# A due-time ranking in the planner, and a down projection that takes two units in turns and reads two PSUM banks at once

## The chip, the cores and the metric

The kernel runs on one core of a Trainium2 chip. The metric is the time of one execution on the device in microseconds (us). Before the change it is 1962.56 us, the median of 3 runs (1949.43 to 1962.99).

## What is computed

One layer of a hybrid decoder, in fp32, for a prompt of 1024 tokens and 8 single-token samples (1032 columns together). Cut to what matters here:

```
h = RMSNorm(x);  q_a, kv_a, g_a, u_c, q_m, g_m = split(h @ w_in)
y_a = (sum of gated compressed, selected and window attention) @ w_o_nsa
y_b = silu(LayerNorm(causal_conv31(glu(u_c)))) @ w_o_conv
y_m = softmax(qm @ k_mem) @ v_mem @ w_o_mem
x   = x + (gm[0]*y_a + gm[1]*y_b + gm[2]*y_m) @ w_out
u, v = split(RMSNorm(x) @ w_ffn_up)             # 1024 -> 2 x 2816
y   = x + (gelu(causal_conv3(u)) * v) @ w_ffn_down   # 2816 -> 1024
```

It returns y for prompt and samples, and the new cache rows and states.

## The kernel before

**Arithmetic.** Every large product is made of three TensorE matmuls: an operand is split into a high and a low part (`wh`, `wl` of a weight; `G1h`, `G1l` and so on of an activation), and `mm3` adds wh·xh, wh·xl and wl·xh in one PSUM bank. A split costs a copy that rounds (`wh`, mostly on ACT) and a subtraction (`wl`, on DVE or POOL). DVE is VectorE, ACT ScalarE, POOL GpSimd, SP the engine that issues most DMAs.

**The planner.** No instruction is issued where it stands in the code. Class `Plan` records each with what it reads and writes (`record`; `record_any` for those that may run on DVE or POOL, or on ACT or POOL), and `flush` places them: a list scheduler with modelled costs. On each engine it looks at the operations that are ready within 30 ns (SP: 60 ns) of the earliest, and takes the one with the lowest `(prio, n)`. `prio` is the number of the instruction in the program, or, in prompt attention, one that a unit was given with a lead. For an operation with a choice of engines, `first` and `finish` choose the engine on which it would end earlier. The model knows that POOL instructions and DVE instructions with two inputs in SBUF keep each other out (`port`, `held`). The engines then run their lists strictly in order. All instructions of the compute engines carry the line of the helper, L95 (`record`) or L126 (`record_any`), so a profile is read by tile names.

**Stages** (us in the profiled execution): norms and input projections to 262; memory attention, compression and the samples' attention to 730; prompt attention to 1002; a reload of three tiles to 1042; output projections to 1240; FFN norm and the start of the up projection to 1306; up projection to 1690; the passage to the down projection to 1717; down projection to 1952; stores to 1959.

**Up and down projection** use Strassen-Winograd products: a unit of output columns is computed by seven products named 1 to 7. In the up projection the 22 units are 11 of `u` (the gate path, whose short convolution and GELU make the tile `ua`) and 11 of `v`. `take_u` does the convolution of a `u` unit on DVE.

**The down projection** has 6 groups of 4, 4, 4, 4, 4 and 2 blocks of the 2816 rows, and in each 4 units of 256 output columns: 24 units, one after the other, with the products in the order "1265734". A product is two pieces of 258 columns, each in a PSUM bank of its own: 6 matmuls to a piece in the first five groups, 3 in the last. Products 1, 6, 7, 4 accumulate in banks A (two pairs in turns), 5 and 3 in B, 2 in C. After each piece an eviction adds its 258 columns to the sum `acc` in SBUF, or, where `acc` is still empty, copies them (ACT). The raw weights of a unit come by one DMA into one of two buffers (`raw_load`), the load for unit n+1 being issued at product 5 of unit n; `w_prep` makes the sums of weight blocks (`s`, `raw<-raw`) and the splits 8 products ahead (`DNL`). Meanwhile `g_prep` makes the 14 tiles G1h to G7l of the next group (1032 columns each) out of `rA` and `rB`, which are read back from DRAM (`gD`), with `tmp` between. At a group's end `xr`, half a tile of the residual, is added to `acc`; in the last group the halves of `acc` go to `o_y`.

Of the kernel before, what the change touches and what calls it, by code (L numbers as in the profile page):

```python
# [2 lines left out]

# [4 lines left out]
F = mybir.dt.float32  # L8
# [12 lines left out]
TH = 516  # L21
# [25 lines left out]
class Plan:  # L47
# [4 lines left out]
           ("PE", "PE"): 0}  # L52

    def __init__(self):
        self.on, self.opt, self.prio, self.count = False, False, None, 0
        self.acc, self.new, self.wait, self.free, self.done = {}, [], {}, {}, []

    @staticmethod
# [3 lines left out]
    def box(self, x):  # L62

        t, ap, off = x.tensor, x.ap, x.offset
        if "DRAM" in str(x.space):
            return t.name, (0, 1, off, off + 1 + sum((n - 1) * abs(s) for s, n in ap)), None
        if t.name not in self.at:
            return t.name, (0, 128, 0, 512), None
        s0 = ap[0][0]
        start, end = self.at[t.name]  # L70
        p, f = off // s0, start + off % s0
        return "sbuf", (p, p + ap[0][1], f, f + 1 + sum((n - 1) * abs(s) for s, n in ap[1:])), (start, end, t.name)
# [20 lines left out]
    def record(self, eng, method, f, a, k):  # L93
        o = Op()
        o.eng, o.fn, o.n, o.opt = eng, (lambda: f(*a, **k)), self.count, self.opt  # L95
        o.prio = self.count if self.prio is None else self.prio
        self.count += 1
        o.deps = {}
        outs = [a[0] if a else k["out"]]
        if "accum_out" in k:  # L100
            outs.append(k["accum_out"])
        if method == "tensor_tensor_reduce":
            outs.append(a[7])
        ins = [x for x in list(a[1:7]) + [v for n, v in k.items() if n not in ("out", "accum_out")] if self.is_ap(x)]
        if "in_offset" in k:
            ins.append(k["in_offset"].ap)
        for x in ins:
            self.touch(o, *self.box(x), False)
        for x in outs:
            self.touch(o, *self.box(x), True)  # L110
        if eng == "PE":
            self.touch(o, "group " + a[0].tensor.name, (0, 1, 0, 1), None, k.get("start", True))
# [15 lines left out]
    def table(self, eng, fn):  # L128

        o = Op()  # L130
        o.eng, o.fn, o.n, o.opt, o.prio, o.deps, o.ns, o.lat, o.alts, o.port = eng, fn, self.count, False, self.count, {}, 1300.0, 0, None, False
        self.count += 1
        self.touch(o, "table", (0, 1, 0, 1), None, True)
        self.new.append(o)
# [35 lines left out]
    def flush(self):  # L170
# [3 lines left out]
        for o in self.new:  # L174
            o.left = len(o.deps)
            for q in o.deps:
                users.setdefault(q, []).append(o)
            if not o.left:
                self.enter(o)
        n = len(self.new)  # L180
        while n:
            best = None
# [29 lines left out]
            for u in users.pop(o, ()):  # L212
                u.left -= 1
                if not u.left:
                    self.enter(u)

    @staticmethod
    def port(e, o):
# [114 lines left out]
class Banks:  # L333


    def __init__(self, pool):
        self.all = [pool.tile([128, 512], F, name=f"bank{i}") for i in range(8)]
        self.turn = {}

    def use(self, **names):  # L340
        self.names = {k: [self.all[i] for i in v] for k, v in names.items()}

    def __call__(self, name):
        i = self.turn.get(name, -1) + 1
# [4 lines left out]
def drain(g):  # L349
    for _ in g:  # L350
        pass
# [33 lines left out]
FP, GSB, OTB, CVP = 0.0, 3, 4, 8e5  # L385
AH, BP = 2.5, 4.0
SLK = {'PE': 30.0, 'ACT': 30.0, 'DVE': 30.0, 'POOL': 30.0, 'SP': 60.0}
GP = (2, 5, 8, 11, 14, 17, 20)
HE, LE, UPL, DNL = "ap", "vp", 3, 8
ORD = (7, 6, 5, 4, 3, 2, 1, 0)  # L390
RB, RW, TB, VB, KH = 3, 3, 2, 2, 'p'
# [2 lines left out]
def _body(tc, nc, d, top):  # L394
# [187 lines left out]
    wo_ids = [add_chunk(d.wo[m], 10) for m in range(8)]  # L582
    wout_ids = [[add_chunk(d.wout[m], 8) for m in range(8)] for _ in range(2)]


    mh = xp_.tile([128, 8, 256], R, name="mh")
    ml = xp_.tile([128, 8, 256], R, name="ml")
# [252 lines left out]
    flush()  # L840
    gp2.close()


    oS = cp.tile([128, NB, 8], F, name="oS")

# [553 lines left out]
    drain(side())  # L1399
    bp.close()  # L1400


    oD = dp.tile([4, 128, T], F, name="oD")
    q4 = Scope(arena, "q4")
# [184 lines left out]
    plan.prio = None  # L1589
    q4.close()  # L1590


    e1, ep = Scope(arena, "e1"), Scope(arena, "ep")
    table("sigmoid_and_others")
# [54 lines left out]
    gp5.close()  # L1649
    e1.close()  # L1650


    xs, wp, xb, us, wx, v1 = [Scope(arena, n) for n in ("x2", "wp", "xb", "us", "wx", "v1")]
    X2 = [xs.tile([128, 8, TH], F, name=f"x2{h}") for h in range(2)]
# [65 lines left out]
    yp.close()  # L1720
    rw.close()

# [17 lines left out]
    units = [("u", p) if v == 0 else ("v", p) for p in range(11) for v in range(2)]  # L1740
    dgroups = [(0, 4), (4, 4), (8, 4), (12, 4), (16, 4), (20, 2)]
    units += [("d", j, p) for j in range(len(dgroups)) for p in range(4)]
    PR, PD = "1267453", "1265734"
    seq = [(n, p) for n in range(2) for p in "12"] + [(0, "6"), (1, "6")] + [(n, p) for n in range(2) for p in PR[3:]]
    seq += [(n, p) for n in range(2, len(units)) for p in (PR if n < NU else PD)]

    def raw_load(n):
        u = units[n]
# [17 lines left out]
    def w_prep(j):  # L1766

        n, p = seq[j]
        if n not in raws:
            raw_load(n)  # L1770
        r = raws[n]
        k = r[0, 0].shape[1]
        s1 = (s1t[n % 2] if n < NU else s1t[0][:, n % 2 * 256:])[:, :k * 128].rearrange("p (c m) -> p c m", m=128)
        if p == "6":
            add(s1, r[1, 0], r[1, 1], OP.add)
            add(r[1, 0], r[0, 0], r[1, 0], OP.subtract)
            add(r[0, 0], s1, r[0, 0], OP.subtract)
        elif p == ("7" if n < NU else "5"):
            if n + 1 < len(units) and n + 1 not in raws:
                raw_load(n + 1)  # L1780
        elif p == "3":
            add(r[0, 1], r[0, 1], r[0, 0], OP.subtract)
        src_ = {"1": r[0, 0], "2": r[0, 1], "6": r[0, 0], "5": s1, "3": r[0, 1], "7": r[1, 0], "4": r[1, 1]}[p]
        if units[n][0] == "d":
            i = wst["slot"]
            wst["slot"] += 1
            i, q = i // 2, i % 2 * 2
        else:
            i, q = wst["slot"] // 2, 0
            wst["slot"] += 2  # L1790
        if i not in slot:
            slot[i] = [rp.tile([128, 4, 128], R, name=nm, bufs=5) for nm in ("wh", "wl")]
        h, l = [x[:, q:q + k] for x in slot[i]]
        split_(h, l, src_)
        w_tiles["s", j] = (h, l)

    def product(j, B, lead):
        n, p = seq[j]
        while wst["prep"] < min(j + lead + 1, len(seq)):
            w_prep(wst["prep"])  # L1800
            wst["prep"] += 1
        wh, wl = w_tiles.pop(("s", j))
        k = wh.shape[1]
        if p == "1":
            bk[n] = {b: [bank(b) for _ in range(2)] for b in "ABC"}
        ps = bk[n][{"1": "A", "6": "A", "7": "A", "4": "A", "5": "B", "3": "B", "2": "C"}[p]]
        for x in range(2):
            o = ps[x][:, :TP_]
            for y in range(k):
                mm3(o, wh[:, y], wl[:, y], B[p][0][:, y, pieces[x]], B[p][1][:, y, pieces[x]],  # L1810
                    y == 0 and p in "152", y == k - 1 and p in "432", skip_group_check=p != "2")
            yield x, o

    bk = {}
    bank.use(A=(0, 1, 2, 3), B=(4, 5), C=(6, 7))
    fs = Scope(arena, "fs")
    FS = fs.tile([128, 22, NB, 3], F, name="FS")
    UO = fs.tile([128, 22, 2], F, name="UO")
# [153 lines left out]
    g_load(0, 1)  # L1972
    drain(g_prep(0))
    j = nup
    for g in range(len(dgroups)):
# [4 lines left out]
        for p in range(4):  # L1980
            for q in range(7):
                if p * 7 + q in GP:
                    next(ahead, None)
                P = seq[j][1]
                for x, ps in product(j, {q: [v[:, :dgroups[g][1] // 2] for v in w] for q, w in GB[g % 2].items()}, DNL):
                    def o(i, h):
                        return acc[2 * p + i][:, h * TH + x * TP_:h * TH + (x + 1) * TP_]
                    t_ = {"1": ((0, 0),), "2": ((0, 0),), "6": ((0, 1),), "7": ((1, 1),), "4": ((1, 0),), "5": ((1, 1),), "3": ((0, 1),)}[P]
                    for i, h in t_:
                        if g == 0 and P in "1654":  # L1990
                            act.activation(o(i, h), ps, AF.Copy)
                        else:
                            vec.tensor_tensor(o(i, h), o(i, h), ps, op=OP.add)
                j += 1
            if p == 3:
                drain(ahead)
            if 0 < g < 5:
                m, h = 2 * p + (g - 1) // 2, (g - 1) % 2
                x_ = xr[p % 2]
# [167 lines left out]
```

## Time and profile before

| | |
|---|---|
| runs | 1949.43, 1962.99, 1962.56 us; median 1962.56 |
| profiled execution | 1960.58 us; its span 1958.8 us; mean granted TensorE clock 0.982 of full speed |
| busy in the span | TensorE 95%, its weight loads 91%, DVE 78%, ACT 47%, POOL 37% |
| chain that ended last, by line | TensorE's own matmuls 36%, DVE's additions into `acc` 3%, no other over 1% |
| DMA | 212.74 MB, 109 GB/s in the mean |

The span is what the profiler saw of one execution, from its first to its last instruction; 1.8 us of that execution's time lie outside it. Busy shares are means over stages with different limits, so the views by stage below say more. In a row, "out<-in" are the program's tile names (numbers left out), "partitions x elements" the size, and a wait in brackets is idle time before an instruction and what ended it.

### The profile page before, as it was taken

What the parts mean: (1) busy time and instruction counts of PE and PEld (TensorE: products, weight loads), DVE (VectorE), ACT (ScalarE), POOL (GpSimd) and SP (SyncE); (2) the same over time, 40 slices, a digit from 0 to 9 for tenths busy, and PEclk for the clock granted to TensorE, in tenths of its full rate; (3) what the DMA queues carried; (4) which work ended last, traced back from release to release, by engine and by line L of the source; (5) the groups of instructions that cost most, each with busy time, mean ns of one, the idle gap of its engine ahead of it and who ended that gap; (6) DMA issues with size and microseconds to landing.
All of it is one profiled execution on the core that took longest, in us unless ns stands there. A gap on an engine that the chain in (4) does not pass through costs nothing. (4 is left out here: it accounts for less than half of the span.)

```text
span 1958.8 us, 36464 instructions
## 1 busy us (share of the span) xinstructions
PE 1861.6 (95%) x13382; PEld 1774.6 (91%) x13382; DVE 1536.2 (78%) x3138; ACT 910.9 (47%) x2073; POOL 718.8 (37%) x796
## 2 busy tenths in 40 slices
PE   7999989999999999999978999899999999998899
PEld 7999989999988678888868999899999999998888
DVE  6499999986675539889865567897766776799998
ACT  7324527424663238888763222533333333453332
POOL 0215725214124534444424554431111211344564
PEclk9999999999899899999989999999999999999999
DMA  7412153324445551111035564132221222233333
GB/s 257 122 57 71 66 190 105 105 90 146 158 140 169 174 156 32 41 47 34 9 129 166 166 227 126 39 109 76 76 98 66 76 76 96 85 137 113 110 91 115
DMA packets 91716, 212.74 MB, mean 109 GB/s; under 512 B 12049, under 2 KB 34265, under 8 KB 89873
## 3 DMA queue, kind: packets, MB, share of 16 engines
q1 hardware_dynamic: 88081, 193.63, 30.4%
q0 software_dynamic: 3456, 16.78, 2.6%
q8 instruction: 105, 1.72, 0.4%
q14 instruction: 74, 0.61, 0.1%
HBM read 161.06 MB, written 53.50 MB: 110 GB/s over the span
## 5 line engine op out<-in xcount | busy, mean ns | idle before, releaser
L95 PE MATMUL bank<-hh,wh 128*128 128x344 f32 x1056 | 346.4, 328 | 7.5 <-ACT cf L95 3.4
L95 PE MATMUL bank<-hh,wl 128*128 128x344 f32 x1056 | 343.1, 325 | 1.2 <-DVE wl L95 1.1
L95 PE MATMUL bank<-hl,wh 128*128 128x344 f32 x1056 | 343.9, 326 | 0.0
L126 ACT ACTIVATE wh<-raw 128x512 fp32r<-128x512 f32 (+2 forms) x255 | 125.5, 508 | 270.6 <-PE bank L95 146.9
L95 PEld LDWEIGHTS bank<-hh,wh 128*128 128x128 f32 x1056 | 201.0, 190 | 12.3 <-ACT gst L95 3.9
L95 PEld LDWEIGHTS bank<-hh,wl 128*128 128x128 f32 x1056 | 201.0, 190 | 4.2 <-DVE wl L95 2.0
L95 PEld LDWEIGHTS bank<-hl,wh 128*128 128x128 f32 x1056 | 201.2, 191 | 1.8 <-issue 0.4
L126 POOL TENSOR_TENSOR wl<-raw,wh 128x256 fp32r<-128x256 f32 (+2 forms) x73 | 81.2, 1117 | 306.6 <-ACT wh L126 280.4
L126 DVE TENSOR_TENSOR wl<-raw,wh 128x512 fp32r<-128x512 f32 (+2 forms) x203 | 125.2, 630 | 46.3 <-ACT wh L126 40.4
L95 DVE TENSOR_TENSOR wl<-wt,wh 128x512 fp32r<-128x512 f32 (+1 forms) x117 | 89.7, 769 | 42.4 <-ACT wh L95 32.2
L95 DVE SCALAR_TENSOR_TENSOR G<-G,vt 128x1024 f32<-128x1024 f32 x90 | 117.7, 1308 | 1.7
L95 DVE TENSOR_TENSOR acc<-acc,bank 128x258 f32<-128x258 f32 x304 | 112.1, 414 | 0.7 <-PE bank L95 0.6
L95 DVE TENSOR_TENSOR pl<-bank,ph 128x512 fp32r<-128x512 f32 (+2 forms) x184 | 100.1, 577 | 11.8 <-ACT ph L95 10.5
L95 POOL TENSOR_SCALAR Pw<-Pw,st,GT 128x64 f32<-128x64 f32 (+5 forms) x128 | 71.8, 577 | 88.3 <-DVE st L95 48.9
L95 PE MATMUL bank<-KK,QS 128*128 128x512 f32 (+3 forms) x384 | 99.7, 356 | 1.1 <-DVE st L95 0.7
L95 POOL TENSOR_TENSOR wl<-wt,wh 128x512 fp32r<-128x512 f32 x35 | 52.0, 1485 | 132.7 <-ACT wh L95 129.7
L95 PE MATMUL bank<-y,wh 128*128 128x258 f32 x512 | 95.0, 282 | 0.0
L95 ACT ACTIVATE ph<-bank 128x512 fp32r<-128x512 f32 (+2 forms) x184 | 85.7, 507 | 18.7 <-PE bank L95 16.5
L95 ACT ACTIVATE wh<-wt 128x512 fp32r<-128x512 f32 x88 | 55.3, 632 | 70.8 <-PE bank L95 67.3
L95 POOL TENSOR_SCALAR wh<-wt 128x512 fp32r<-128x512 f32 (+1 forms) x64 | 44.4, 698 | 98.8 <-PE bank L95 96.3
L95 PEld LDWEIGHTS bank<-y,wh 128*128 128x128 f32 x512 | 79.8, 189 | 0.0
L95 PE MATMUL bank<-y,wl 128*128 128x258 f32 x256 | 72.3, 283 | 0.0
(552 smaller groups left out, 6440.0 us busy)
## 6 DMA issues: line engine op xcount, KB each, us to landing
wt<-in_w_in SPq DMA_DIRECT2D x88, 256.0 KB
raw<-in_wup SPq DMA_DIRECT2D x44, 512.0 KB
gmD<-gst SPq DMA_DIRECT2D x72, 172.0 KB
g<-gmD SPq DMA_DIRECT2D x24, 516.0 KB
gD<-ua SPq DMA_DIRECT2D x22, 516.0 KB
raw<-in_wdn SPq DMA_DIRECT2D x20, 512.0 KB
wt<-in_wout SPq DMA_DIRECT2D x32, 256.0 KB
rA<-gD SPq DMA_DIRECT2D x5, 1032.0 KB
```

The source lines that it names most:

```text
L95: o.eng, o.fn, o.n, o.opt = eng, (lambda: f(*a, **k)), self.count, self.opt
L126: o.alts[eng] = ((lambda f=f, a=a, k=k: f(*a, **k)),) + self.cost(eng, method, a, k, outs, ins) + (self.shared(eng, method, outs, ins),)
```

## The change

Three things are changed.

1. `deadlines`, called at the start of each `flush`, gives every operation a time at which it is due: a matmul at the sum of the modelled durations of the matmuls before it in the old ranking, any other operation so much earlier than its users as it takes itself with the hand-over. Operations without users are due 20 us after the end. With `EDF = 0` all operations recorded from the input projections on are ranked by that time. The optional fillers (pieces of the convolution and gate projections with priorities from 8e5) keep their places, put on the same scale.
2. PSUM is allotted as four tiles of two banks. The planner now separates uses of a tile by bank.
3. The down projection takes two units in turns: `PAIR` names product and unit of 14 steps. An eviction is one instruction that reads both banks of a product, 516 columns. First sums (16) are copied by ACT whichever product they are. The raw load of unit n+2 is issued after the last split of unit n; at the last up unit two units are loaded.

```diff
+EDF = 0
+PAIR = [(int(x[1]), x[0]) for x in "10 11 20 60 61 50 21 70 71 30 40 51 41 31".split()]
...
+            f = off % ap[0][0]
+            return t.name, (0, 128, f // 512 * 512, (f + sum((n - 1) * abs(s) for s, n in ap[1:])) // 512 * 512 + 512), None
...
+        o.edf = self.edf and not self.opt
...
+    def deadlines(self, users):
+
+        t = 0.0
+        for o in sorted((o for o in self.new if o.eng == "PE" and not o.opt), key=lambda o: (o.prio, o.n)):
+            o.due = t
+            t += o.ns
+        end = t + 20000.0
+        for o in reversed(self.new):
+            ns = min(a[1] for a in o.alts.values()) if o.alts else o.ns
+            lat = max(a[2] for a in o.alts.values()) if o.alts else o.lat
+            d = getattr(o, "due", end)
+            for u in users.get(o, ()):
+                raw = u.deps[o]
+                if u.eng == o.eng and not raw:
+                    d = min(d, u.due - ns)
+                else:
+                    d = min(d, u.due - lat - self.LAT.get((o.eng, u.eng), 200) - ns)
+            o.due = d
...
+            if o.edf:
+                o.prio = o.due
+            else:
+                i = bisect.bisect_left(ks, o.prio)
+                o.prio = ts[i] if i < len(ks) else end + o.prio
...
-        self.all = [pool.tile([128, 512], F, name=f"bank{i}") for i in range(8)]
+        self.pairs = [pool.tile([128, 2, 512], F, name=f"bank{i}") for i in range(4)]
+        self.all = [self.pairs[i // 2][:, i % 2] for i in range(8)]
...
-    PR, PD = "1267453", "1265734"
+    PR = "1267453"
...
-    seq += [(n, p) for n in range(2, len(units)) for p in (PR if n < NU else PD)]
+    seq += [(n, p) for n in range(2, NU) for p in PR]
+
+    seq += [(n + i, p) for n in range(NU, len(units), 2) for i, p in PAIR]
...
-        elif p == ("7" if n < NU else "5"):
-            if n + 1 < len(units) and n + 1 not in raws:
-                raw_load(n + 1)
+        elif p == "7" and n < NU:
+            for ahead in (n + 1,) if n < NU - 1 else (n + 1, n + 2):
+                if ahead not in raws:
+                    raw_load(ahead)
...
+        if n >= NU and p == "43"[n % 2] and n + 2 < len(units):
+            raw_load(n + 2)
...
-            bk[n] = {b: [bank(b) for _ in range(2)] for b in "ABC"}
+            bk[n] = {b: bank(b) for b in "ABC"}
...
-            yield x, o
+            if units[n][0] != "d":
+                yield x, o
+            elif x:
+                yield 2, ps[:, :, :TP_]
...
-    bank.use(A=(0, 1, 2, 3), B=(4, 5), C=(6, 7))
+    bank.use_pairs(A=(0, 1), B=(2,), C=(3,))
...
+            for _, ps in product(j, {q: [v[:, :dgroups[g][1] // 2] for v in w] for q, w in GB[g % 2].items()}, DNL):
+                i, h = {"1": (0, 0), "2": (0, 0), "6": (0, 1), "7": (1, 1), "4": (1, 0), "5": (1, 1), "3": (0, 1)}[P]
+                o = acc[2 * p + i][:, h * TH:(h + 1) * TH].rearrange("p (x t) -> p x t", x=2)
+                if (p, i, h) not in written:
+                    written.add((p, i, h))
+                    act.activation(o, ps, AF.Copy)
+                else:
+                    vec.tensor_tensor(o, o, ps, op=OP.add)
```

What becomes of the instructions' order is seen best at three places. (In the changed kernel the helpers' lines are L97 and L130.)

On DVE in the down projection (`bank_60` to `bank_67` are the eight banks before, `bank_60` to `bank_63` the four pairs now: A, A, B and C; the number behind `acc` tells which tile), a piece before, where the splits of weights needed eight products later stand among the evictions in the order of the program:

```order
L95 TENSOR_TENSOR acc_301_379<-acc_301_379,bank_60 128x258
L126 TENSOR_TENSOR s_279_357<-raw_282_360 128x256
L126 TENSOR_TENSOR wl_115<-raw_282_360,wh_114 128x256
L126 TENSOR_TENSOR wl_117<-raw_282_360,wh_116 128x256
L95 TENSOR_TENSOR acc_301_379<-acc_301_379,bank_61 128x258
L126 TENSOR_TENSOR raw_282_360<-raw_282_360 128x2x128
L95 TENSOR_TENSOR acc_301_379<-acc_301_379,bank_66 128x258
L126 TENSOR_TENSOR raw_282_360<-s_279_357,raw_282_360 128x2x128
L95 TENSOR_TENSOR acc_301_379<-acc_301_379,bank_67 128x258
L126 TENSOR_TENSOR G1l_390<-rA_376,G1h_389 128x1032
```

and a piece of the same stage now:

```order
L97 TENSOR_TENSOR acc_308_382<-acc_308_382,bank_61 128x516
L97 TENSOR_TENSOR acc_305_379<-acc_305_379,bank_62 128x516
L130 TENSOR_TENSOR rA_372<-rB_373,tmp_374 128x2x516
L97 TENSOR_TENSOR acc_306_380<-acc_306_380,bank_60 128x516
L130 TENSOR_TENSOR wl_97<-raw_281_355,wh_96 128x256
L97 TENSOR_TENSOR acc_308_382<-acc_308_382,bank_62 128x516
L130 TENSOR_TENSOR G5l_396<-rA_372,G5h_395 128x1032
L97 TENSOR_TENSOR acc_308_382<-acc_308_382,bank_61 128x516
L130 TENSOR_TENSOR raw_282_356<-s_279_353,raw_282_356 128x2x128
L97 TENSOR_TENSOR acc_307_381<-acc_307_381,bank_62 128x516
```

Each eviction is one instruction of 516 columns, and one other instruction at most stands between two of them here; instructions of 1032 columns are still among these. Over the stage DVE has 152 evictions of 516 columns in place of 304 of 258 (1717 to 1952 us holds 293 of them); 25 subtractions of 256 columns (`wl`) and 10 sums of weight blocks have gone from DVE to POOL, and 3 instructions of 1032 columns from POOL to DVE.

On ACT at the first units of the up projection, before (`ua` is the GELU, `uS` an eviction):

```order
L95 ACTIVATE ua_370<-ua_370 128x1032
L126 ACTIVATE wh_102<-s_279_357 128x512
L95 ACTIVATE uS_277_355<-bank_60 128x258
L95 ACTIVATE uS_277_355<-bank_61 128x258
L95 ACTIVATE ua_372<-ua_372 128x1032
L126 ACTIVATE wh_114<-raw_281_359 128x512
L126 ACTIVATE wh_104<-raw_281_359 128x512
```

and now:

```order
L97 ACTIVATE uS_277_351<-bank_60 128x258
L130 ACTIVATE wh_98<-s_279_353 128x512
L97 ACTIVATE uS_277_351<-bank_60 128x258
L130 ACTIVATE wh_100<-raw_281_355 128x512
L97 ACTIVATE uS_277_351<-bank_60 128x258
L130 ACTIVATE wh_110<-raw_283_357 128x512
L97 ACTIVATE uS_277_351<-bank_60 128x258
L97 ACTIVATE uS_278_352<-bank_60 128x258
L97 ACTIVATE ua_366<-ua_366 128x1032
```

The first GELU now stands behind the evictions into `uS` and the weight splits between them.

On SP in the last group, before:

```order
L95 DMA raw_282_360<-in_wdn 128x1024
L95 DMA raw_281_359<-in_wdn 128x512
L95 DMA xr_388<-xD 128x516
L95 DMA raw_282_360<-in_wdn 128x512
L95 DMA raw_281_359<-in_wdn 128x512
L95 DMA o_y<-acc_301_379 128x516
L95 DMA raw_282_360<-in_wdn 128x512
```

and now:

```order
L97 DMA xr_383<-xD 128x516
L97 DMA o_y<-acc_301_375 128x516
L97 DMA o_y<-acc_303_377 128x516
L97 DMA o_y<-acc_302_376 128x516
L97 DMA raw_281_355<-in_wdn 128x512
L97 DMA raw_282_356<-in_wdn 128x512
L97 DMA o_y<-acc_301_375 128x516
```

The last two raw loads now stand behind three stores, the third of which can start when product 7 of the group's first unit has been added (step 8 of 14).

## Rows read from the trace of the kernel before

**Rows 1.** The page's busy time, share of the span and instructions of each engine.

```profile
PE 1861.6 (95%) x13382; PEld 1774.6 (91%) x13382; DVE 1536.2 (78%) x3138; ACT 910.9 (47%) x2073; POOL 718.8 (37%) x796
```

**Rows 2.** Windows by stage: window, us, then each engine's busy us, clock, DMA.

```profile
core 0: us, PE busy (x) PEld busy (x) DVE busy (x) ACT busy (x) POOL busy (x), PEclk, DMA share, GB/s
...
215.00:262.00 47.00, 39.57 (x226) 37.61 (x225) 45.64 (x88) 18.06 (x38) 28.91 (x28) 0.93 0.29 99
...
730.00:1002.00 272.00, 266.45 (x1848) 234.97 (x1846) 238.66 (x866) 228.19 (x644) 127.98 (x198) 1.00 0.14 38
...
1240.00:1306.00 66.00, 56.71 (x436) 54.95 (x435) 58.94 (x93) 33.63 (x65) 33.64 (x17) 0.95 0.15 47
1306.00:1690.00 384.00, 384.00 (x3202) 383.94 (x3200) 281.28 (x494) 143.24 (x281) 71.86 (x46) 1.00 0.25 85
1690.00:1717.00 27.00, 22.04 (x163) 21.11 (x162) 22.82 (x32) 14.38 (x28) 10.61 (x10) 0.94 0.26 84
1717.00:1952.00 235.00, 218.28 (x1756) 212.37 (x1755) 232.24 (x496) 90.81 (x203) 121.77 (x127) 1.00 0.34 113
```

**Rows 3.** TensorE's waits, 1717 to 1952 us: waiter, releaser, total us, times, longest.

```profile
PE bank L95 <- DVE acc L95: 16.2, 19, 2.5
```

**Rows 4.** DVE's groups, 1717 to 1952 us: count, busy us, mean ns, idle before.

```profile
L95 DVE TENSOR_TENSOR acc<-acc,bank 128x258 f32<-128x258 f32 x293 | 108.0, 413 | 0.7 <-PE bank L95 0.6
L126 DVE TENSOR_TENSOR wl<-raw,wh 128x256 fp32r<-128x256 f32 x85 | 48.0, 594 | 0.0
L126 DVE TENSOR_TENSOR raw<-raw 128x256 f32<-128x256 f32 x25 | 12.7, 508 | 0.1
...
L126 DVE TENSOR_TENSOR G5l<-rA,G5h 128x1032 fp32r<-128x1032 f32 x5 | 7.2, 1444 | 0.0
```

**Rows 5.** POOL's groups in the same window.

```profile
L126 POOL TENSOR_TENSOR wl<-raw,wh 128x256 fp32r<-128x256 f32 x27 | 28.9, 1079 | 25.1 <-ACT wh L126 18.6 <-DVE wl L126 4.9 <-PE bank L95 1.3
```

**Rows 6.** Timeline of a wait in the down projection: start, duration, instruction, idle before.

```profile
1778.74 3.36 POOL L126 TENSOR_TENSOR G3l<-rB,G3h 128x1032 fp32r<-128x1032 f32 x1
...
1779.80 2.58 DVE L126 TENSOR_TENSOR raw<-s,raw 128x256 f32<-128x256 f32 x1
...
1782.30 0.74 DVE L95 TENSOR_TENSOR acc<-acc,bank 128x258 f32<-128x258 f32 x2
...
1782.77 0.39 PE L95 MATMUL bank<-G7h,wh 128*128 128x258 f32 x1 [2.46 <-DVE acc L95]
1782.97 0.41 DVE L126 TENSOR_TENSOR wl<-raw,wh 128x256 fp32r<-128x256 f32 x1
```

**Rows 7.** Timeline of DVE back to back: at 1786 us, and at 1258 us.

```profile
1786.23 2.41 DVE L95 TENSOR_TENSOR acc<-acc,bank 128x258 f32<-128x258 f32 x7
...
1258.39 0.68 DVE L126 TENSOR_TENSOR B6l<-t,B6h 128x516 fp32r<-128x516 f32 x1
1259.00 0.68 DVE L126 TENSOR_TENSOR t<-x,x 128x516 f32<-128x516 f32 x1
```

**Rows 8.** DVE's groups over the whole span: the commonest that reads 512 columns of PSUM.

```profile
L95 DVE TENSOR_TENSOR pl<-bank,ph 128x512 fp32r<-128x512 f32 x112 | 73.6, 683 | 8.0 <-ACT ph L95 6.9 <-DVE st L95 0.2
```

**Rows 9.** Timeline of the raw loads in the down projection: issue, and first use.

```profile
1729.54 0.34 SPq L95 DMA_DIRECT2D raw<-in_wdn  x1
...
1733.24 1.03 POOL L126 TENSOR_TENSOR s<-raw 128x256 f32<-128x256 f32 x1 [3.02 <-DMA raw<-in_wdn]
```

**Rows 10.** TensorE's longest wait in 1690 to 1717 us.

```profile
PE bank L95 <- ACT v L95: 2.4, 1, 2.4
```

**Rows 11.** TensorE's longest waits in 1240 to 1306 us, and ACT there.

```profile
PE bank L95 <- ACT wh L126: 3.8, 2, 2.2
...
1303.28 1.06 ACT L95 ACTIVATE ua<-ua 128x1032 f32<-128x1032 f32 x1 [2.10 <-DVE ua L95]
```

**Rows 12.** TensorE's longest wait in 215 to 262 us.

```profile
PE bank L95 <- ACT cf L95: 3.4, 1, 3.4
```

**Rows 13.** Timeline of POOL in 1240 to 1306 us, among DVE's instructions with two inputs in SBUF.

```profile
1260.98 9.55 POOL L126 TENSOR_TENSOR x<-x,t 128x516 f32<-128x516 f32 x1 [5.54 <-DVE x L126]
```

More of the change, by code (lines that the diff above doesn't have):

```diff
@@ L1 @@
+import bisect
 import math
@@ L54, in __init__ @@
     def __init__(self):
-        self.on, self.opt, self.prio, self.count = False, False, None, 0
+        self.on, self.opt, self.prio, self.count, self.edf = False, False, None, 0, False
         self.acc, self.new, self.wait, self.free, self.done = {}, [], {}, {}, []
@@ L67, in box @@
         if t.name not in self.at:
-            return t.name, (0, 128, 0, 512), None
+            f = off % ap[0][0]
+            return t.name, (0, 128, f // 512 * 512, (f + sum((n - 1) * abs(s) for s, n in ap[1:])) // 512 * 512 + 512), None
         s0 = ap[0][0]
@@ L111, in record @@
         if eng == "PE":
-            self.touch(o, "group " + a[0].tensor.name, (0, 1, 0, 1), None, k.get("start", True))
+            name, b, _ = self.box(a[0])
+            self.touch(o, "group " + name, b, None, k.get("start", True))
         if method == "activation" and a[2] not in (AF.Copy, AF.Square):
@@ L130, in table @@
         o = Op()
+        o.edf = False
         o.eng, o.fn, o.n, o.opt, o.prio, o.deps, o.ns, o.lat, o.alts, o.port = eng, fn, self.count, False, self.count, {}, 1300.0, 0, None, False
@@ L179, in flush @@
                 self.enter(o)
+        self.deadlines(users)
         n = len(self.new)
@@ L215, in flush @@
                     self.enter(u)
+    def deadlines(self, users):
[15 more added lines that the diff above has]
+            o.due = d
+        ks, ts, t = [], [], 0.0
+        for o in sorted((o for o in self.new if o.eng == "PE" and not o.opt), key=lambda o: (o.prio, o.n)):
+            t += o.ns
+            ks.append(o.prio)
+            ts.append(t)
+        for o in self.new:
+            if o.edf:
[3 more added lines that the diff above has]
+                o.prio = ts[i] if i < len(ks) else end + o.prio
     @staticmethod
@@ L341, in use, with use_pairs @@
         self.names = {k: [self.all[i] for i in v] for k, v in names.items()}
+    def use_pairs(self, **names):
+        self.names = {k: [self.pairs[i] for i in v] for k, v in names.items()}
     def __call__(self, name):
@@ L583, in _body @@
     wout_ids = [[add_chunk(d.wout[m], 8) for m in range(8)] for _ in range(2)]
+    plan.edf = EDF <= 0
     mh = xp_.tile([128, 8, 256], R, name="mh")
@@ L841, in _body @@
     gp2.close()
+    plan.edf = EDF <= 1
     oS = cp.tile([128, NB, 8], F, name="oS")
@@ L1400, in _body @@
     bp.close()
+    plan.edf = EDF <= 2
     oD = dp.tile([4, 128, T], F, name="oD")
@@ L1590, in _body @@
     q4.close()
+    plan.edf = EDF <= 3
     e1, ep = Scope(arena, "e1"), Scope(arena, "ep")
@@ L1650, in _body @@
     e1.close()
+    plan.edf = EDF <= 4
     xs, wp, xb, us, wx, v1 = [Scope(arena, n) for n in ("x2", "wp", "xb", "us", "wx", "v1")]
@@ L1721, in _body @@
     rw.close()
+    plan.edf = EDF <= 5
     xt = Scope(arena, "xt")
@@ L1804, in product @@
         if p == "1":
-            bk[n] = {b: [bank(b) for _ in range(2)] for b in "ABC"}
+            bk[n] = {b: bank(b) for b in "ABC"}
         ps = bk[n][{"1": "A", "6": "A", "7": "A", "4": "A", "5": "B", "3": "B", "2": "C"}[p]]
         for x in range(2):
-            o = ps[x][:, :TP_]
+            o = ps[:, x, :TP_]
             for y in range(k):
@@ L1974, in _body @@
     j = nup
+    written = set()
     for g in range(len(dgroups)):
@@ L1979, in _body @@
         ahead = g_prep(g + 1) if g + 1 < len(dgroups) else iter(())
[L1980 to L1995, printed above, removed]
+        left = {p: 7 for p in range(4)}
+        for i28 in range(28):
+            if i28 in GP:
+                next(ahead, None)
+            n, P = seq[j]
+            p = units[n][2]
+            for _, ps in product(j, {q: [v[:, :dgroups[g][1] // 2] for v in w] for q, w in GB[g % 2].items()}, DNL):
[6 more added lines that the diff above has]
+                    vec.tensor_tensor(o, o, ps, op=OP.add)
+            j += 1
+            left[p] -= 1
+            if i28 == 26:
                 drain(ahead)
+            if left[p]:
+                continue
             if 0 < g < 5:
```

## The prediction

> **What bounds the kernel now.** I read the busy shares first: TensorE works 95% of the span [rows 1], so only its gaps can be won, 97 us of 1958.8 (1958.8 − 1861.6). The windows by stage say where they are [rows 2]. In the up projection 3202 matmuls fill 384.00 us: 0.12 us each with no gap, the price of a matmul of 258 columns. The down projection has 1756 of them, 1756 × 0.12 = 210.7 us of work in a window of 235, so 24.3 us are lost there, the largest loss in any stage that the change rewrites. DVE is busy 232.24 of these 235 us, and TensorE's waits in this window name DVE's additions into `acc`: 16.2 us in 19 waits, the longest 2.5 [rows 3]. So here DVE, not TensorE, sets the pace. Smaller gaps by the same count: the passage before it, 163 × 0.12 = 19.6 of 27, 7.4 lost; the start of the up projection, 436 × 0.12 = 52.3 of 66, 13.7 lost; 215 to 262 us, 47 − 39.57 = 7.4 idle; prompt attention 272 − 266.45 = 5.5. The clock is at or near full speed in all of them, so I count nothing for it.
>
> **Part 1, the eviction of two banks.** DVE drops 304 additions of 258 columns for 152 of 516; ACT's share (32 pieces, now 16) was not what TensorE waited for. Seven evictions back to back end after 2.41 us, one alone takes 0.41, so the step is (2.41 − 0.41) / 6 = 0.333 us; DVE instructions of 516 columns start 0.61 us apart [rows 7]. A pair saves 2 × 0.333 − 0.61 = 0.056, 152 pairs 8.5 us. That row reads SBUF, the new instruction PSUM. The nearest row with PSUM has 0.683 us for 512 columns [rows 8]; with that as the step a pair costs 0.017 more and the stage 2.6. The other end takes the mean of 0.413 for the single eviction [rows 4]: 2 × 0.413 − 0.61 = 0.216, 33 us. I take 8.5, since the backlogged case is the one that delays TensorE. [...]
>
> **Part 2, work handed from DVE to POOL.** By the order, 25 subtractions of 256 columns and 10 sums of blocks leave DVE, 3 instructions of 1032 columns come to it. An undisturbed one of 256 columns takes 0.41 us [rows 6], the mean in this stage is 0.594 and 0.508 [rows 4]: the rest is waiting for POOL, as the timeline shows, where a POOL instruction of 3.36 us lies over a DVE one that took 2.58, the evictions behind it came late, and TensorE waited 2.46 [rows 6]. At 0.41 the 35 save 14.4, the three cost 3 × 1.44 = 4.3 [rows 4]. POOL works longer (35 × 1.08 = 38 us, less three long ones) [rows 5], but DVE has fewer instructions that can meet it: of 256 columns 137 before and 102 now on DVE, 64 and about 99 on POOL, products 8,800 and 10,100. I charge 2 us for that, and the sum is −8. Bounds: −15 (at the means), and +14 (POOL's added 29 us all in DVE's way, less 15).
>
> **Part 3, rank and turns.** DVE's work falls to 232.2 − 8.5 − 8 = 215.7 us, 5.0 above TensorE's 210.7, and with 2.8 us of idle time as before the stage would be about 218.5. The rank puts evictions ahead of splits that are due eight products later, as the piece of DVE's order shows, so what is left should lie behind TensorE. One new tight place comes: bank pair B is used by products 5 and 3 with a single product of the other unit between, 12 × 0.12 = 1.44 us in which the matmuls end and a 0.61 us eviction must start and finish. It fails when a DVE instruction of 1.2 to 1.4 us is just running. Twenty such places, half of them late by 0.7, make 7 us, a part of the 7.8 (218.5 − 210.7) that I already left; in the last group the product between is half as long and 4 places cost 0.4 each, 1.6. So waits of 24.3 become 9.4: **−15**. Bounds: −24 (all gone) and +13 (245 us of DVE's work, rival C).
>
> **Part 4, SP.** Each raw load waits for the last split of its buffer and takes 3.7 us from issue to use (1729.54 to 1733.24) [rows 9]; with splits 8 products ahead, 11.5 us, that is hidden. In the last group it is not: the loads for the last two units stand behind the store that waits for step 8 of 14. From there six half products remain, 6 × 0.72 = 4.3 us, against about 0.8 for the eviction, 3.7 for the load and 1 for the split: **+1.2** (0 to +4; at +4 nothing else hides it). The 14 stores behind it go out later than before only by that.
>
> **Part 5, other stages.** The passage had one wait of 2.4 us for an eviction on ACT [rows 10]; eviction now goes first, but two units must be loaded and split in front of the down projection: −2 (+3 to −5). At the start of the up projection a weight split came late by 3.8 us in two waits, with GELUs of 1.06 us in front [rows 11], and these stand behind it now: −3 (+2 to −9). At 215 us a copy on ACT held TensorE for 3.4 [rows 12]: −2 (+3 to −5). Attention is reordered thoroughly on DVE and ACT, but has 5.5 us to lose at most and is bound by TensorE: 0 (+10 to −5). Matmuls, weights and loaded bytes are the same, and up projection and reload keep nearly their order: 0.
>
> Sum: −15 + 1.2 − 2 − 3 − 2 = −20.8 on the profiled 1960.58 us, which stands 2.0 below the median of the three runs. That is **1940 us**.
>
> **Rivals.**
> *A, the rank empties the gaps everywhere* (0.17). For it: nearly all the waits named are instructions that were ready but stood behind less urgent ones. Against: the ranks rest on modelled times, and a list in strict order can't correct a wrong one. Down −21, passage −5, start of up −8, 215 us −5, attention −5: −44, 1916.
> *B, the two-bank eviction gives DVE nothing and pair B takes the old wait's place* (0.27). For it: the 0.683 us from PSUM [rows 8], and 24 tight places where there were none as tight (before, a piece had a whole product, and its first piece half a product more). DVE falls to 232.2 + 2.6 − 8 = 226.8, the stage to 229.6, and waits for B of 24 × 0.7 = 17 us agree with that: −5; other stages −4: 1952.
> *C, DVE and POOL block each other* (0.11), slower. POOL's added 29 us stand wholly in DVE's way, which then has 215.7 + 29 = 245 us: the stage gets 10 + 2.8 longer, and reordered attention loses up to 10: about 1980 with no gain elsewhere, 1973 with the 7 of part 5. It decides from the point where blocking exceeds 235 − 218.5 = 16.5 us. For it: the 2.58 us of rows 6, and a POOL instruction of 516 columns that took 9.55 us beside a busy DVE [rows 13]. Against: in that row POOL, not DVE, was held up, and the planner models the exclusion. [...]
> That the change does not do what it says, a false wait between the two banks of a tile, I count in B: each piece of order shows single evictions in step with their products.
>
> **Chances and range.** Forecast 0.45, A 0.17, B 0.27, C 0.11. A measurement of this kernel tells 1% from no change, so faster is below 1942.9 and slower above 1982.2. The forecast's own range (1930 to 1950, from the bounds of parts 1 and 5) lies about two thirds below 1942.9: 0.29 + 0.17 of A + 0.02 of B = 0.48 faster; C gives 0.07 slower; the rest 0.45. The range leaves out the lower half of A and most of C: 1917 to 1963.
>
> **What would show it.** Right: the down projection's window about 220 us with DVE's share under 98%, the two-bank eviction's step near 0.61 us, waits for `acc` under 10 us and mostly at the second use of pair B, one wait of 1 us for `wh` in front of the last two units, and attention's window within 3 us of 272. B shows as a step of 0.69 and many waits of 0.7 before product 3; C as DVE's subtractions at 0.8 us or more in the mean, with DVE still full. The prediction is wrong if a stage that I set to 0 moves by more than 5 us, above all attention, where the ranks changed most and I had no row to price them.

## The result: 460 us slower, and none of it where the work was changed

The changed kernel takes 2420.97 us (median of 4 runs, 2417.61 to 2423.78) against 1962.78 before (1949.43 to 1963.73). The ratio is 1.235, 95% interval 1.2303 to 1.2397. The forecast was 1940 with a range to 1963, so it was wrong by 480 us.

The page of the changed kernel, its line of busy time (columns as in [rows 1]):

```profile
PE 2046.2 (85%) x13382; PEld 1828.2 (76%) x13382; DVE 1522.8 (63%) x2996; ACT 932.9 (39%) x2066; POOL 676.3 (28%) x777
```

The same 13382 matmuls, and every engine has a smaller share of the span than in [rows 1]: nothing is full, so something waits. The lengths of the stages, each from its first matmul to the first of the next (the first stage from the start of the span, the last to the last matmul), read from the traces of before, of the changed kernel and of four experiments told below:

```
us                              before  changed    e1      e4      e9     e10
projections                      294.2    338.5   344.4   289.9   291.1   289.2
memory, compression, samples     435.0    543.7   536.8   432.4   432.3   425.2
prompt attention                 280.6    410.9   395.9   282.0   281.4   282.1
reload, output projection 1      133.0    154.7   154.3   132.9   133.4   130.6
output projection 2               99.5    112.3   112.1   100.7   102.8   103.2
up projection                    462.1    612.4   595.7   455.9   455.0   454.3
passage and down projection      249.7    242.2   292.0   240.4   247.0   232.1
```

Six stages that the change only reorders lose 468 us together. The one that it rewrites gains 7. Windows of the changed kernel (columns as in [rows 2]): attention, the middle of the up projection, the down projection.

```profile
882.00:1293.00 411.00, 331.85 (x1894) 263.67 (x1892) 253.46 (x874) 240.99 (x650) 132.49 (x201) 0.91 0.12 33
...
1620.00:2160.00 540.00, 444.14 (x3273) 403.81 (x3272) 294.00 (x545) 151.58 (x290) 30.51 (x24) 1.00 0.19 62
2178.00:2412.00 234.00, 224.50 (x1806) 219.62 (x1805) 221.19 (x340) 97.34 (x208) 135.82 (x136) 0.99 0.35 117
```

The up projection is the plainest: in [rows 2] 3202 matmuls took 384.00 us without a gap; here 3273 take 540 at the same clock, and no other engine is busy more than 55%. In attention the granted clock fell too, from 1.00 to 0.91. TensorE's waits in the stretch that holds the up projection, 1560 to 2172 us (waiter, releaser, total us, times, longest):

```profile
PE bank L97 <- ACT uS L97: 30.9, 65, 0.5
PE bank L97 <- ACT v L97: 26.2, 55, 0.5
PE bank L97 <- DVE uS L97: 21.8, 41, 1.2
PE bank L97 <- DVE v L97: 19.7, 38, 0.6
PE bank L97 <- DVE ua L97: 5.2, 9, 0.6
```

`uS`, `v` and `ua` are the evictions of that stage. 208 waits for an eviction, nearly all of 0.5 us, in a stage that had none in its steady part. One of them in the timeline (start, duration, instruction, idle before):

```profile
1800.04 0.28 PE L97 MATMUL bank<-B7h,wl 128*128 128x258 f32 x1
...
1800.16 0.29 PE L97 MATMUL bank<-B7h,wh 128*128 128x258 f32 x1
...
1800.29 0.28 PE L97 MATMUL bank<-B7l,wh 128*128 128x258 f32 x1
1800.61 0.39 ACT L97 ACTIVATE uS<-bank 128x258 f32<-128x258 f32 x1 [1.33 <-PE bank L97]
...
1801.04 0.39 PE L97 MATMUL bank<-B7h,wl 128*128 128x258 f32 x1 [0.47 <-ACT uS L97]
```

The first row is the last matmul of a product's first piece, in one bank. The next two belong to the second piece, in the other bank. Then TensorE stops in the middle of that piece until ACT has emptied the first bank, which the second piece does not use. And ACT itself started late, only when the two matmuls into the bank that it does not read had ended. From the second to the third matmul of the piece it is 0.75 us instead of 0.12.

**What happened.** Semaphores are not written by hand here; the tile framework inserts them by comparing what instructions read and write. The planner's `box` (the function that says which part of a tile an instruction uses) was taught to tell the two banks of a tile apart, the framework was not: in this program it orders two uses of one PSUM tile whichever bank they touch. So wherever the two banks of a pair are used one by one (every stage but the down projection) evictions and matmuls wait for each other without need. In the built program each semaphore wait can be followed to the instruction that raises the semaphore. Where that instruction shares with the waiting one nothing but a PSUM tile, of which they use different banks, the wait is false (counted are the waits that the waiting instruction itself carries):

```
false waits                                 matmul on ACT, DVE    ACT, DVE on matmul
before, e2, e3                                    0                     0
changed kernel                              356 + 237 = 593       256 + 200 = 456
e1 (before, with two-bank tiles only)       380 + 256 = 636       260 + 325 = 585
e4 (changed, banks declared apart)                0                     0
e7 (only matmuls freed)                           0               257 + 167 = 424
e8 (only evictions freed)                   359 + 234 = 593             0
```

Where an instruction has several waits, the framework puts some of them into a wait instruction just in front of it. With these the changed kernel has 672 and 728 false waits, e1 756 and 877, e7 0 and 728, e8 676 and 0, and the others still none. Yet fewer of TensorE's instructions carry a wait than before, 1803 weight loads for 2096 in the traces: the number of waits says nothing, their place does.

### The profile page after: what moved, and what is told of

The parts are those of the page before. It is cut to its first block, busy times and chain, and to the rows that moved or that the text cites. A ratio compares the mean times of both kernels' runs of the same rounds, so it can differ in the third digit from the quotient of the medians.

```text
span 2419.1 us, 36234 instructions
## 1 busy us (share of the span) xinstructions
PE 2046.2 (85%) x13382; PEld 1828.2 (76%) x13382; DVE 1522.8 (63%) x2996; ACT 932.9 (39%) x2066; POOL 676.3 (28%) x777
## 4 chain that ended last, share of the span: by engine, by line
PE 38%; DVE 8%; ACT 3%; issue 2%; DMA 2%; POOL 1%; SPq 0%; DVEq 0%; ACTq 0%; POOLq 0%
PE bank L97 38%; DVE acc L97 1%; ACT uS L97 1%; ACT v L97 1%; POOL wl L130 1%; DVE v L97 1%; DVE uS L97 1%; DVE pl L97 1%; DVE wl L130 1%; DMA raw<-in_wdn 0%; DMA rA<-gD 0%; ACT ph L97 0%; DVE yz L97 0%; DVE Pw L97 0%; DVE x L130 0%
## 5 line engine op out<-in xcount | busy, mean ns | idle before, releaser
L97 PE MATMUL bank<-hh,wl 128*128 128x344 f32 x1056 | 340.2, 339 | 33.6 <-ACT gst L97 16.8
L97 PE MATMUL bank<-hl,wh 128*128 128x344 f32 x1056 | 341.1, 338 | 21.6 <-ACT gst L97 12.4
L97 PE MATMUL bank<-hh,wh 128*128 128x344 f32 x1056 | 341.7, 338 | 20.2 <-ACT zS L97 7.7
L130 ACT ACTIVATE wh<-raw 128x512 fp32r<-128x512 f32 (+2 forms) x264 | 129.1, 504 | 369.1 <-PE bank L97 248.4
L97 PEld LDWEIGHTS bank<-hh,wl 128*128 128x128 f32 x1056 | 203.4, 196 | 52.6 <-ACT gst L97 24.9
L97 PEld LDWEIGHTS bank<-hl,wh 128*128 128x128 f32 x1056 | 204.7, 197 | 34.2 <-ACT gst L97 17.0
L97 PEld LDWEIGHTS bank<-hh,wh 128*128 128x128 f32 x1056 | 204.4, 196 | 33.7 <-ACT zS L97 11.6
L130 DVE TENSOR_TENSOR wl<-raw,wh 128x512 fp32r<-128x512 f32 (+2 forms) x201 | 129.9, 650 | 114.1 <-ACT wh L130 108.7
L130 POOL TENSOR_TENSOR s<-raw 128x256 f32<-128x256 f32 (+2 forms) x24 | 33.8, 1408 | 417.1 <-DVE wl L130 349.3
L97 DVE TENSOR_TENSOR pl<-bank,ph 128x512 fp32r<-128x512 f32 (+2 forms) x184 | 103.9, 581 | 71.7 <-PE bank L97 42.8
L97 ACT ACTIVATE ph<-bank 128x512 fp32r<-128x512 f32 (+2 forms) x184 | 91.1, 511 | 100.9 <-PE bank L97 86.1
L97 DVE TENSOR_TENSOR wl<-wt,wh 128x512 fp32r<-128x512 f32 (+1 forms) x117 | 81.6, 701 | 75.8 <-ACT wh L97 62.9
L97 PE MATMUL bank<-KK,QS 128*128 128x512 f32 (+3 forms) x384 | 119.4, 390 | 11.4 <-DVE st L97 6.6
L97 POOL TENSOR_SCALAR Pw<-Pw,st,GT 128x64 f32<-128x64 f32 (+5 forms) x128 | 72.9, 585 | 186.6 <-DVE st L97 171.3
L97 DVE SCALAR_TENSOR_TENSOR G<-G,vt 128x1024 f32<-128x1024 f32 x90 | 120.0, 1333 | 1.8
L130 POOL TENSOR_TENSOR wl<-raw,wh 128x256 fp32r<-128x256 f32 (+2 forms) x75 | 73.3, 988 | 124.3 <-ACT wh L130 121.8
L97 PE MATMUL bank<-y,wh 128*128 128x258 f32 x512 | 97.4, 285 | 7.2 <-DVE x L97 7.2
L97 DVE TENSOR_TENSOR acc<-acc,bank 128x516 f32<-128x516 f32 x152 | 100.7, 680 | 3.4 <-PE bank L97 2.5
L97 ACT ACTIVATE wh<-wt 128x512 fp32r<-128x512 f32 x88 | 55.1, 630 | 105.2 <-PE bank L97 88.5
L97 POOL TENSOR_TENSOR wl<-wt,wh 128x512 fp32r<-128x512 f32 x35 | 48.9, 1396 | 159.2 <-ACT wh L97 111.1
L97 PEld LDWEIGHTS bank<-y,wh 128*128 128x128 f32 x512 | 79.6, 189 | 10.1 <-DVE x L97 10.1
L97 PEld LDWEIGHTS bank<-KK,QS 128*128 128x128 f32 x384 | 68.9, 206 | 23.7 <-DVE st L97 10.8
```

The lines of the kernel that those rows point to most:

```text
L130: o.alts[eng] = ((lambda f=f, a=a, k=k: f(*a, **k)),) + self.cost(eng, method, a, k, outs, ins) + (self.shared(eng, method, outs, ins),)
```

## The experiments

The theories were: (1) false waits between the banks of a tile; (2) the rank by due times spoils the engines' order; (3) the chip itself holds TensorE up while a neighbouring bank is read.

**e1, two-bank tiles alone.**

```diff
 (before)
-        self.all = [pool.tile([128, 512], F, name=f"bank{i}") for i in range(8)]
+        self.pairs = [pool.tile([128, 2, 512], F, name=f"bank{i}") for i in range(4)]
+        self.all = [self.pairs[i // 2][:, i % 2] for i in range(8)]
```
(and `box` by bank, as in the change)

> The kernel before with one edit: PSUM is allotted as four tiles of two banks and used bank by bank as before (no rank, no turns, no two-bank eviction). Theory 1 (false waits: whoever inserts the semaphores orders uses of one tile, whichever bank they touch, so a matmul into one bank waits for the eviction of the other): 2350 to 2480 us, with waits of about 0.5 us for ACT and DVE evictions in the middle of a product's second piece, as in the changed kernel. Theory 2 (the rank by due times spoils the order of the engines): 1950 to 1970 us, as before.

Measured: 2436.67 us (2433.1 to 2439.49), ratio to before 1.243, interval 1.2381 to 1.2479. The allotment alone costs all of it, and in the down projection 42 us more, where it still evicts bank by bank (waits for `acc`, 16.2 us in 19 waits in [rows 3]):

```profile
PE bank L96 <- DVE acc L96: 32.8, 53, 2.2
```

**e2, the rank alone, and e3, rank and turns with single banks.**

```diff
 (e2: before)
+        self.deadlines(users)          # and EDF = 0, as in the change
 (e3: the changed kernel)
-        self.pairs = [pool.tile([128, 2, 512], F, name=f"bank{i}") for i in range(4)]
-        self.all = [self.pairs[i // 2][:, i % 2] for i in range(8)]
+        self.all = [pool.tile([128, 512], F, name=f"bank{i}") for i in range(8)]
...
-    bank.use_pairs(A=(0, 1), B=(2,), C=(3,))
+    bank.use(A=(0, 1, 2, 3), B=(4, 5), C=(6, 7))
```

> The kernel before with one edit: the rank by due times in all stages; single-bank tiles, one unit after the other, evictions of 258 columns. Theory 1: 1935 to 1965 us (some gain in the down projection, nothing else). Theory 2: 2300 us or more.

> The changed kernel with eight tiles of one bank again, and so two evictions of 258 columns for each product; rank and turns stay. Theory 1: 1935 to 1960 us. Theory 2: 2300 us or more.

Measured: e2 1949.11 us (ratio 0.995, interval 0.9927 to 0.9973), e3 1943.72 (0.9917, 0.989 to 0.9945). Theory 2 falls: the rank costs nothing, it gains some 10 us (1959.54 before in that session).

**e4, the changed kernel with its banks declared apart.** After each instruction is issued, the framework is told that it needs no wait for earlier ones of other engines that use the other bank of its tile, unless the planner (exact by bank) has a dependence between the two.

```diff
-            o.fn()
+            self.apart(o, o.fn())
...
+    def apart(self, o, r):
+        for name, b in o.banks:
+            near = self.near.setdefault(name, [])
+            for q, c, x in near:
+                if q.eng != o.eng and q not in o.deps and (c[3] <= b[2] or b[3] <= c[2]):
+                    self.tc.declare_no_dep(r.ins, x, reason="other bank")
+            near.append((o, b, r.ins))
+            del near[:-80]
```

> The changed kernel whole (rank, turns, two-bank tiles and evictions), but of every two instructions that use different banks of one tile, and nothing else in common, it is declared that the one needs no wait for the other. Theory 1: the 460 us come back, and what is left is what the prediction summed: 1917 to 1963, likeliest 1940. Theory 2: still 2300 or more. A third way (the chip itself holds TensorE up while another engine reads a neighbouring bank of the same pair): also 2300 or more, with TensorE's gaps in place but without a semaphore that ends them.

Measured: 1934.46 us (1929.93 to 1940.21), ratio to before 0.9863, interval 0.9823 to 0.9903. Run once more (e11) it gave 1938.16, ratio 0.9893, interval 0.9857 to 0.9928:

> The kernel of e4 once more, on the same chip as e9 and e10 and sharing their runs of the kernel before: 1930 to 1940 us, ratio 0.982 to 0.990.

All 460 us come back and some 25 more (the kernel before had 1959.54 us in e4's session, 1962.32 in e11's). Theory 3 falls with it: matmuls go into one bank while the other bank of the pair is emptied, at full pace (0.12 to 0.13 us from one to the next in the rows below; 390 us / 3250 = 0.12 in the up projection's window). A place like the one above, in e4's timeline:

```profile
1503.19 0.28 PE L97 MATMUL bank<-B7h,wl 128*128 128x258 f32 x1
...
1503.31 0.28 PE L97 MATMUL bank<-B7h,wh 128*128 128x258 f32 x1
...
1503.43 0.29 PE L97 MATMUL bank<-B7l,wh 128*128 128x258 f32 x1
...
1503.51 0.39 ACT L97 ACTIVATE uS<-bank 128x258 f32<-128x258 f32 x1 [0.65 <-PE bank L97]
1503.56 0.29 PE L97 MATMUL bank<-B7h,wl 128*128 128x258 f32 x1
```

The eviction starts 0.32 us after the start of its piece's last matmul (0.57 in the changed kernel), and the third matmul of the next piece 0.13 after the second. e4's windows, attention, up and down:

```profile
722.00:1004.00 282.00, 268.14 (x1894) 241.29 (x1893) 242.85 (x875) 232.11 (x649) 132.51 (x201) 0.98 0.17 47
1300.00:1690.00 390.00, 389.96 (x3250) 389.75 (x3249) 286.91 (x538) 149.65 (x290) 25.95 (x23) 1.00 0.27 85
1700.00:1932.00 232.00, 222.76 (x1802) 217.79 (x1802) 222.01 (x339) 96.38 (x207) 133.15 (x136) 1.00 0.36 119
```

TensorE has no gap in the up projection again, and attention has its clock nearly back (0.98).

**e7 and e8, one direction of the waits at a time.**

```diff
 (e4)
-                if q.eng != o.eng and q not in o.deps and (c[3] <= b[2] or b[3] <= c[2]):
+                if o.eng == "PE" != q.eng and q not in o.deps and (c[3] <= b[2] or b[3] <= c[2]):            # e7
+                if o.eng != "PE" and q.eng != o.eng and q not in o.deps and (c[3] <= b[2] or b[3] <= c[2]):  # e8
```

> The changed kernel where a matmul need not wait for an engine that uses the other bank of its tile, while an eviction still waits for matmuls already issued into the other bank (466 such waits stay in the program, of 1,070). If TensorE's loss is the matmuls' own waits: 1935 to 1990 us, since evictions come 0.2 to 0.5 us late, which one product of slack hides. If the evictions' lateness is what costs (buffers come free late all along): 2200 or more.

> The counterpart of e7: an eviction need not wait for matmuls into the other bank, but a matmul still waits for the eviction of the other bank (593 waits). If the matmuls' own waits are the loss: 2150 to 2400 us, somewhat less than the changed kernel, since each eviction starts some 0.2 us earlier. If the evictions' lateness is the loss: 1935 to 2000.

Measured, one run each: e7 2007.65 us, e8 2116.93. (The counts in the expectation of e7 were taken another way than the table above, in which 424 false waits of evictions stay in e7 for 456 in the changed kernel, and all 728 with the separate wait instructions.) Both lie outside what was expected: e7 is 18 us above its band, and e8 33 below. Against e4 the late evictions alone cost 73 us, the matmuls' waits alone 182, and together 486: they feed each other. In the up projection this is plainest: 456.6 us in e7, 534.2 in e8, 612.4 with both, against 455.9 in e4. Late evictions alone cost nothing there; e7's 73 us lie mostly in the memory stage (466.9 us for 432.4) and in attention (304.2 for 282.0). In e8's waits one sees how:

```profile
PE bank L97 <- ACT uS L97: 11.6, 53, 0.2
```

The mean wait is 0.22 us, in the changed kernel 0.48 (30.9 / 65). An eviction that is free to go starts while TensorE still does the two matmuls; one that waits for them starts 0.25 us later (0.57 less 0.32, the timelines of the changed kernel and of e4), and TensorE stands for all of it (that this is the whole of the difference is argued, not shown).

**e5, e6, e9, e10: what the parts are worth without the false waits.** All are e4 with one edit.

```diff
-EDF = 0
+EDF = 6                                   # e5: no rank;  e6: EDF = 5, rank in up and down alone
...
-    seq += [(n + i, p) for n in range(NU, len(units), 2) for i, p in PAIR]
+    seq += [(n, p) for n in range(NU, len(units)) for p in "1265734"]    # e9
...
-PAIR = [(int(x[1]), x[0]) for x in "10 11 20 60 61 50 21 70 71 30 40 51 41 31".split()]
+PAIR = [(int(x[1]), x[0]) for x in "10 11 20 60 50 61 21 30 70 71 51 40 41 31".split()]   # e10
```
(e9 also issues the raw load of unit n+2 at product 4 of every unit)

> The kernel of e4 with the rank off in every stage (turns and two-bank evictions alone, banks apart). If the prediction's parts hold, the down projection keeps about 9 us of its gain and the other stages lose theirs (the 10 us that the rank alone brought in e2): 1945 to 1953 us. Rival (the rank is what lets DVE's evictions through in time, turns without it bring nothing): 1957 to 1965.

> The kernel of e4 with the rank in the up and down projections alone. If the rank gains at the start of the up projection and in the down projection, 1936 to 1942 us; if it gains in the stages before, as part 5 of the prediction has for 215 to 262 us, 1940 to 1948; in e4 the stages before the up projection were 4.5 us shorter than before the change.

> The kernel of e4 with one unit after the other in the down projection, products in the old order 1265734; rank and two-bank evictions stay. Every accumulating bank pair is then used again after a single product, 4 places in each of 24 units, 96 in place of 24. By the price that part 3 of the prediction put on such a place (half of them late by 0.7 us) the down projection loses 25 us more: 1955 to 1962 us. Rival (the two units in turns bring nothing, the rank alone keeps evictions in time): 1933 to 1940.

> The kernel of e4 with the two units' products interleaved so that every bank pair has at least two products between its uses (1u 1v 2u 6u 5u 6v 2v 3u 7u 7v 5v 4u 4v 3v): no tight place at pair B is left. If the waits for additions into acc that remained in e4 (7.8 us in 11 waits) come from pair B: 1927 to 1932 us. If they come from DVE's being full (222 us busy of 232): no change, 1933 to 1938.

Measured: e5 1957.5 us (ratio 0.9987, interval 0.9968 to 1.0006), e6 1947.79 (0.9926, 0.9909 to 0.9943), e9 1944.95 (0.9898, 0.9866 to 0.9929), e10 1927.87 (0.9839, 0.9805 to 0.9874). TensorE's waits for `acc`, in the order e5, e9, e4, e10, e3 (a row from each):

```profile
PE bank L97 <- DVE acc L97: 12.3, 12, 2.1
```
```profile
PE bank L97 <- DVE acc L97: 11.6, 7, 3.5
```
```profile
PE bank L97 <- DVE acc L97: 7.8, 11, 2.3
```
```profile
PE bank L97 <- DVE acc L97: 3.0, 5, 0.9
```
```profile
PE bank L97 <- DVE acc L97: 2.6, 6, 0.9
```

e5: without the rank, turns and two-bank evictions bring nothing that can be told from zero. The rival of that expectation holds; the down projection shortens by 2 us instead of 9. e6: the rank in the stages before the up projection is worth 10 to 13 us (1947.79 against 1934.46 and 1938.16), the upper expectation. e9: one unit after the other loses 7 to 10 us at the medians, outside both expectations; but its interval and e11's (0.9857 to 0.9928, same session) overlap almost wholly, so the loss rests on the stage, 247.0 us for 240.4 (e4) and 237.9 (e11). There e9's granted clock was 0.97 (1708 to 1941 us) and e4's 1.00, so not all of it need be the order. e4 and e11 are one program, and their 2.5 us of difference in this stage say how far such figures can be trusted. e10: with two products between all uses of a bank pair the waits for `acc` fall to 3.0 us (16.2 in [rows 3]), the stage to 232.1 and the kernel to 1927.87, the fastest here (against e11 of the same session 1938.16, with intervals that overlap slightly; the stage's own length and its waits say the same). Neither the rank alone (passage and down 254.9 us in e2), nor turns and evictions alone (247.8 in e5) gains what both do (240.4 and 237.9). Rank and turns with single-bank evictions have 243.9 (e3).

## Why the prediction was wrong, point by point

**The step that failed** is the last sentence of the rivals: "That the change does not do what it says, a false wait between the two banks of a tile, I count in B: each piece of order shows single evictions in step with their products." The pieces of order show instructions, not what they wait for, and the one on evictions was from the down projection, the only stage where a pair is emptied whole. The consequence was priced with pair B's 17 us in one stage; it was 593 waits of matmuls (672 with the separate wait instructions) in all the others. With it fell "Matmuls, weights and loaded bytes are the same, and up projection and reload keep nearly their order: 0" (they lost 150 and 22) and the 0 for attention (+130). The condition named last, a stage set to 0 that moves by more than 5 us, was what came.

Its order of size could have been estimated had the wait been assumed. The up projection has 22 units of 7 products, 308 pieces evicted one by one. If each second one holds the matmuls up for the eviction and its hand-over (0.39 us, and 0.36 around it, times read from the changed kernel's timeline, less the 0.12 of a step), that is, as an estimate, 154 × 0.63 = 97 us there; 208 waits came, 131 us by the same step, of 150 lost. The remaining 19 were not traced.

**Where the false waits are taken away, the total held, and its parts only in some.** Against 1940, e4 has 1934.46 and e11 1938.16, and by their traces:
- Part 1: two evictions back to back take 1.28 us in e4, one 0.68 (the mean of 149):

```profile
1731.64 1.28 DVE L97 TENSOR_TENSOR acc<-acc,bank 128x516 f32<-128x516 f32 x2
```

so the step is 0.60; 0.61 was taken and not the 0.69 of rival B. e4 stands 9.3 us below e3 at the medians, 8.5 was forecast, though the intervals of these two overlap. In the stage itself the two-bank eviction brings 3.5 us (e4) or 6.0 (e11) over e3's 243.9, and e3's waits for `acc` were the shorter (2.6 us against 7.8): what DVE saves reaches TensorE only in part, and the 8.5 is not shown as a gain of the stage.
- Part 2: DVE's subtractions take what they took, and are fewer ([rows 4] had 85 of 594 ns):

```profile
L131 DVE TENSOR_TENSOR wl<-raw,wh 128x256 fp32r<-128x256 f32 x59 | 34.0, 585 | 4.5 <-ACT wh L131 4.5
```

so POOL's added work did not stand in DVE's way more than before, and rival C is out. A window of e4 with as many matmuls as [rows 2] has for the down projection (1759 for 1756):

```profile
1708.00:1933.40 225.40, 216.35 (x1759) 211.97 (x1757) 214.92 (x335) 90.56 (x197) 128.34 (x133) 1.00 0.36 119
```

DVE is busy 214.9 us there; 215.7 was the sum.
- Part 3 was too hopeful: in the same window 225.4 − 1759 × 0.12 = 14.3 us are still lost (12.1 in e11, over its last 1756 matmuls), 9.4 was forecast; passage and down projection gain 9.3 (e4) and 11.7 (e11) for the 15.8 of the sum (15 − 1.2 + 2). The place was right in kind: e10, which loosens pair B, gains 8.3 and 5.8 us more in that stage (against e4 and e11), and 8.6 had been put on it. The price of a place was not: e9's 72 added places should have cost 25 us and cost 7 to 9, e9's lower clock included. Why a tight place costs 0.3 us in one order and 0.1 in the other stays open.
- Part 4: after 1900 us e4 has no wait for `wh` over 0.20 us; 1.2 was forecast, 0 was the bound.
- Part 5: projections −4.2 and −4.7 (−2 forecast), up projection −6.3 and −6.4 (−3), attention +1.4 and +1.0 (0); the memory stage, not forecast, −2.6 and −5.3, output projection 2 +1.2 and +3.4. Most of e4's gain outside the down projection is larger than forecast, and makes good what the down projection lacks; that the total agrees to 6 us is partly luck.

## What to carry to other kernels

A tile is the unit in which whoever inserts semaphores may think: joining two buffers into one tile for the sake of one instruction can make other instructions, which use the two apart and have nothing to do with each other, wait for each other, in every stage that shares the allotment. Look, in the built program, at what the waits of a steady, gapless stage wait for, and not at how many there are, before setting such a stage to zero. And waits inserted on both sides cost far more here than the sum of the two sides (73, 182, 486 us; one run each of the first two).

## What the runs showed of the hardware

TensorE's granted clock fell in prompt attention, where the false waits broke up its work: 0.91 over the stage (1.00 in [rows 2], 0.98 in e4, 0.99 in e7 and in e8), and 0.77 in one stretch of it, a mean over the two levels that the trace has there, 1.0 and 0.5 of full speed:

```profile
1200.00:1260.00 60.00, 49.91 (x252) 40.05 (x251) 31.67 (x106) 29.41 (x78) 14.66 (x23) 0.77 0.02 5
```

In the middle of the up projection, where TensorE's waits were about as long (0.50 us in the mean, 0.49 in attention) and its busy share the same (444 of 540 us, 82%, against 332 of 411, 81%), the clock stayed at 1.00; what makes the difference no run here shows. VectorE reads two banks of PSUM with one instruction at 0.60 us for 516 columns (the second of two back to back in e4), where two instructions took 0.67 (2 × 0.333, from the seven back to back in [rows 7]).
